# Strassen products from the third retention unit on instead of the fifth, with the first group's rows staged in DRAM

## The chip, the core and the metric

One Trainium2 chip; the program runs on one of its cores. The metric is the device time of one execution in microseconds (us). TensorE (PE) multiplies, VectorE (DVE) and ScalarE (ACT) work on the results, GpSimd (POOL) does a few small operations, and the queue of SyncE (SP) issues nearly all DMAs, in order.

## The reference, cut to what matters

A decoder trunk of two layers on x (2048 rows of 1024, float32). The first layer is gated retention with 4 heads, the second is sliding-window attention with sinks on one shared K/V. The change touches the first layer's input projection alone:

```python
def retention_layer(x, g_norm, w_in, w_out, sin, cos):
    proj = rmsnorm(x, g_norm) @ w_in
    q, k, v, gate = jnp.split(proj, [D_MODEL, 2 * D_MODEL, 2 * D_MODEL + RET_V_TOTAL], axis=-1)
    ...
    o = rms(retention(q, k, v))
    o = o.reshape(b, s, RET_V_TOTAL) * jax.nn.silu(gate)
    return x + o @ w_out
```

Per head q and k are 256 wide, v and the gate 512 wide each. `rms` makes o independent of a row's scale but for its EPS.

## The kernel before, in words

Every product is made of three: both operands are split into a high part (a cast to fp32r) and a low part (the rest), and hi·hi, hi·lo and lo·hi are summed in PSUM. ACT makes the high part and DVE the low part (`wload`, L118, for weights). A weight piece is 128 x 1024 floats, 512 KB.

`phase_a` is the retention layer. The rows lie in 4 groups of 512, and a *unit* is one group and one head, so there are 16 units, u0 to u15; u0 to u3 are the first group. The loop at its end (L802) puts `main(u+1)` (the projections of the next unit), `ret(u)` (the retention of this one) and `out_a(u)` (its share of the output product) side by side; `drive` steps two of them in a fixed ratio.

`main` computes q and k (`project_qk`, 96 matmuls of 512 columns), then v and the gate in one of two ways:

- A *plain* unit, u < PLAIN (`plain_vg`): 4 pieces for v and 4 for the gate, each used by 24 matmuls, 192 in all. The rows are not normalised; a row's scale is applied when the result leaves PSUM (`vs`, `es`, and the scale of Silu).
- A *Strassen* unit (`strassen`, L420): the 1024 x 1024 weight block and the rows are cut in 2 x 2 blocks and 7 products stand in for 8. There are 14 pieces, each used by 12 matmuls, 168 in all. Four of the seven products take sums of weight blocks (T1 to T4), and four take sums of row blocks (S1 to S4).

These sums are made beforehand, staged in DRAM, and read back:

- `stage_sums(h)` (L359) makes T1 to T4 of a head, in 4 blocks. A block loads 4 tiles (L368), subtracts and adds on DVE (L371 to L374) and writes 4 tiles (L376).
- `stage_rows(g)` (L306) makes a group's normalised rows and S1 to S4: one small product spreads the rows' scales (L315), then 4 blocks follow, each 2 tile loads (L323), 2 multiplications (L327), 4 additions of half width (L331 to L334) and 6 writes.
- `row_stats(g)` (L289) makes the scales. `load_rows` and `load_sums` read the staged rows back and split them (L345 to L347).

All tiles of the staging come from one ring of six (`stp`, tag "st"). The generators are queued in `behind`, and `step()`, called at fixed places of the projections, advances the first of them. Weights and everything that is read back share a ring of three raw tiles and rings of three for the high and low parts.

The program's order on each engine is made by a scheduler when it is built, so staging can stand earlier than the step that asked for it. After phase_a comes phase_b, the attention layer, which the change leaves alone.

Of the kernel before, what the change touches and what calls it, by code (L numbers as in the profile page):

```python
# [24 lines left out]
RH = 4  # L25
# [9 lines left out]

PSUM_BUFS = {"rr": 4, "s": 2, "f": 2}
RAW = 3
PLAIN = 4
SX = ("S2", "S3", "S1", "S4")
ST = ("T2", "T3", "T1", "T4")  # L40

# [16 lines left out]
def tile_yoco(ctx, tc, x, x_t, w_qk, w_vg, wo_a, w_kv, w_b, wo_b, ag, kvg, bg, kng, qng,  # L58
# [208 lines left out]
    def phase_a(pa):  # L267
# [8 lines left out]
        st = {}  # L276
        behind = []

        def step():
            if behind and next(behind[0], "end") == "end":  # L280
                behind.pop(0)
# [67 lines left out]
        def load_rows(g, kp):  # L349
            if kp == 0:  # L350
                st["next"] = xt_tiles(f"a{g}")
            load_part(st["next"][0][kp], st["next"][1][kp], st["rows", g][kp], f"{g}_{kp}")

        def load_sums(g, n):
            hi, lo = (xsp.tile([P, KT // 2, H], F32R, tag=f"x{hl}{n}", name=f"x{hl}_{g}_{n}") for hl in ("hi", "lo"))
            load_part(hi, lo, st["rsums", g][n], f"{g}_{n}")
            st["sum", n] = hi, lo
# [115 lines left out]
        def main(u):  # L473
            g, h = units[u]
            n = f"a{u}"
            plain = u < PLAIN
            if h == 0:
                cs = p1.tile([P, T], F32, tag="cos", name=f"cos_{n}")
                sn = p1.tile([P, T], F32, tag="sin", name=f"sin_{n}")
                st["trig"] = [cs, sn]  # L480

                def load_trig():
                    nc.sync.dma_start(cs, cos_t[:, g * T : (g + 1) * T])
                    nc.sync.dma_start(sn, sin_t[:, g * T : (g + 1) * T])

                if u:
                    load_trig()
            cs, sn = st["trig"]
            q = p1.tile([P, 2, T], F32, tag="q", name=f"q_{n}")
            k = p1.tile([P, 2, T], F32, tag="k", name=f"k_{n}")  # L490
            vhi, vlo, gate = [None] * MT, [None] * MT, [None] * MT

            def put_v(m, src, scale):
                vhi[m] = vp.tile([P, DV], F32R, tag="vhi", name=f"vhi_{n}_{m}")
                vlo[m] = vp.tile([P, DV], F32R, tag="vlo", name=f"vlo_{n}_{m}")
                nc.scalar.mul(vhi[m], src, scale)
                nc.vector.scalar_tensor_tensor(vlo[m], src, scale, vhi[m].bitcast(F32), op0=ALU.mult, op1=ALU.subtract)

            def put_gate(m, src, scale=1.0):
                gate[m] = gp.tile([P, DV], F32, tag="gate", name=f"gate_{n}_{m}")  # L500
                nc.scalar.activation(gate[m], src, AF.Silu, scale=scale)

            if h == 0:
                st["xt"] = st.pop("next", None) or xt_tiles(n)
            xt = st["xt"]
            yield from project_qk(u, xt, q, k, load_trig if u == 0 else None)
            if plain:
                yield from plain_vg(u, xt, put_v, put_gate)
            else:
                if h == 0:  # L510
                    load_sums(g, SX[3])

                def src(p):
                    name = (None, None, "T2", "T3", "T1", None, "T4")[p]
                    w = st["sums", h][name] if name else w_vg[(h,) + ((0, 0), (1, 0), 0, 0, 0, (1, 1))[p]]
                    return [w[0], w[1]]

                def evac(i, j, f, src):
                    if j:
                        put_gate(2 * i + f, src)  # L520
                    else:
                        put_v(2 * i + f, src, vd[:, h : h + 1])

                def after(p):

                    if h == RH - 1 and g + 1 < NG:
                        if p in (1, 2, 6):
                            for kp in {1: (0,), 2: (1,), 6: (2, 3)}[p]:
                                load_rows(g + 1, kp)
                        elif p:  # L530
                            load_sums(g + 1, SX[p - 3])

                yield from strassen(f"{n}v", src, xt, evac, after)
                st["es", u] = [ep[:, h : h + 1]] * MT
            st[u] = (q, k, vhi, vlo, gate, st.pop(("es", u)))
# [52 lines left out]
        def plain_vg(u, xt, put_v, put_gate):  # L588
            g, h = units[u]
            n = f"a{u}"  # L590
            xhi, xlo = xt
            last = u == PLAIN - 1
            if u == 0:
                behind.insert(0, row_stats(0))
            vs = small.tile([P, MT], F32, tag="vs", bufs=2, name=f"vs_{n}")
            es = small.tile([P, MT], F32, tag="es4", bufs=2, name=f"es_{n}")
            st["es", u] = [es[:, c : c + 1] for c in range(MT)]

            def evac_v(m, ps):
                if m == 0:  # L600

                    ms, rx = st["stats", g]
                    nc.gpsimd.tensor_tensor(vs, rx, rx, op=ALU.mult)
                    nc.gpsimd.tensor_scalar(vs, vs, vd[:, h : h + 1], None, op0=ALU.mult)
                    nc.gpsimd.tensor_scalar(es, ms, ep[:, h : h + 1], None, op0=ALU.mult)
                put_v(m, ps, vs[:, m : m + 1])

            def before_v(kp):
                step()
                if last:  # L610
                    load_sums(1, SX[kp])

            def before_g(kp):
                step()
                if last and kp:
                    load_rows(1, kp - 1)

            yield from proj(vg_pieces(h, 0), KT, xhi, xlo, False, evac_v, f"{n}v", before=before_v)
            yield from proj(vg_pieces(h, 1), KT, xhi, xlo, False,
                            lambda m, ps: put_gate(m, ps, st["stats", g][1][:, m : m + 1]), f"{n}g", before=before_g)  # L620
            if last:
                load_rows(1, 3)

        def vg_pieces(h, j):
            return [w_vg[h, kp // 2, j, kp % 2] for kp in range(KT // 2)]
# [172 lines left out]
        for _ in main(0):  # L798
            pass
        bias = bias_rows()  # L800
        todo = list(pieces_b())
        for u in range(nu - 1):  # L802

            g, h = units[u + 1]
            if u + 1 in (1, 4, 5, 6):
                behind.append(stage_sums({1: 0, 4: 1, 5: 2, 6: 3}[u + 1]))
            if h == 2 and g + 1 < NG:
                behind.append(row_stats(g + 1))
                behind.append(stage_rows(g + 1))
            if u + 1 in (8, 9, 10, 12, 13, 14):  # L810
                behind.append(stage_b(todo[:9]))
                del todo[:9]
            drive(tc, main(u + 1), ret(u), 2 if u + 1 < PLAIN else 3, 0)
            for _ in itertools.islice(bias, 2 if u >= RH else 0):
                pass
            if u < nu - 2:
                for _ in out_a(u):
                    pass
# [484 lines left out]
```

## Time and profile before

| what | value |
|---|---|
| median of 3 runs (lowest to highest) | 2477.26 us (2474.19 to 2480.29) |
| the profiled execution's own time | 2477.26 us |
| its span in the profile | 2475.5 us |
| PE busy | 2418.5 us, 11576 matmuls, 98% of the span |
| DVE busy | 1624.1 us, 66% |
| ACT busy | 1055.0 us, 43% |
| DMA moved | 499.97 MB, mean 202 GB/s |
| granted TensorE clock | 0.993 of full speed |

Busy shares are means over stages. A matmul's busy time is pipelined with the next one's, so what a matmul costs is read from the spacing of their starts. Times of rows are counted from the span's start.

### The profile page before, as it was taken

How to read it: one execution, taken by the hardware profiler on the slowest of the kernel's cores; microseconds unless marked ns; L12 is line 12 of the kernel's file. 1: busy time of each engine (PE TensorE's matmuls, PEld its weight loads, DVE VectorE, ACT ScalarE, POOL GpSimd, SP SyncE). 2: the span in 40 equal slices, each digit the busy share in tenths (PEclk: the TensorE clock that was granted, in tenths of full speed). 3: DMA queues.
4: the chain of work that ended last, by engine and by line, in shares of the span. 5: the costliest groups of instructions: out<-in, count | busy, mean ns of one | idle time of the engine just before them, and what ended most of it. 6: DMA issues, size and time to landing. Idle time of an engine off the chain costs nothing.

```text
span 2475.5 us, 32133 instructions
## 1 busy us (share of the span) xinstructions
PE 2418.5 (98%) x11576; PEld 1965.9 (79%) x11576; DVE 1624.1 (66%) x2898; ACT 1055.0 (43%) x2028; POOL 234.6 (9%) x288
## 2 busy tenths in 40 slices
PE   8999999999999999999999999999999999999997
PEld 6888778887878888887788888887687787777776
DVE  5546665787778668588667765744656566566665
ACT  4333233543536455355455543433424334334332
POOL 0000000110001020001002000022101101102010
PEclk9999999999999999999999999999999999999998
DMA  8433843589786477498548843646554674655661
GB/s 297 141 116 128 285 136 115 187 310 322 228 285 218 129 255 265 134 309 296 160 153 292 290 128 94 207 149 220 192 204 147 231 239 136 211 201 184 201 216 69
DMA packets 178075, 499.97 MB, mean 202 GB/s; under 512 B 20363, under 2 KB 32956, under 8 KB 177916
## 3 DMA queue, kind: packets, MB, share of 16 engines
q1 hardware_dynamic: 177836, 497.66, 59.8%
q8 instruction: 91, 1.49, 0.2%
q14 instruction: 68, 0.56, 0.1%
q0 software_dynamic: 80, 0.26, 0.0%
HBM read 396.11 MB, written 104.88 MB: 202 GB/s over the span
## 4 chain that ended last, share of the span: by engine, by line
PE 54%; DVE 4%; DMA 3%; ACT 1%; SPq 0%; issue 0%; POOL 0%; ACTq 0%; DVEq 0%; POOLq 0%
PE o_t L1117 3%; PE pp_ao L146 2%; PE pp_ao L147 2%; PE pp_ao L148 2%; PE s_t L1068 2%; PE pp_bo L256 2%; PE pp_bo L255 2%; PE pp_bo L257 2%; PE pT_t L1099 1%; PE qtp_b L963 1%; DVE P_t L1071 1%; DMA wlo<-in_w_b 1%; PE ot_r L726 0%; PE o_r L698 0%; PE o_r L700 0%; PE o_r L699 0%
## 5 line engine op out<-in xcount | busy, mean ns | idle before, releaser
L146 PE MATMUL pp_ao<-ohi_r,whi_ao 128*128 128x512 f32 x512 | 198.8, 392 | 6.5 <-ACT whi_ao L125 5.5
L147 PE MATMUL pp_ao<-olo_r,whi_ao 128*128 128x512 f32 x512 | 199.6, 390 | 0.0
L148 PE MATMUL pp_ao<-ohi_r,wlo_ao 128*128 128x512 f32 x512 | 194.2, 390 | 0.9 <-DVE wlo_ao L126 0.9
L1071 DVE CUSTOM_DVE_ANT_0 P_t<-s_t,bias,nsnk 128x256 f32<-128x256 f32 (+1 forms) x256 | 115.1, 472 | 89.7 <-PE s_t L1068 80.1
L1081 ACT ACTIVATE P_t<-P_t,nm_t 128x128 f32<-128x128 f32 x256 | 100.4, 394 | 117.2 <-DVE P_t L1078 114.9
L766 DVE TENSOR_TENSOR x_r<-x_r,pp_ao 128x512 f32<-128x512 f32 x128 | 86.4, 683 | 63.7 <-PE pp_ao L148 63.4
L114 POOL TENSOR_SCALAR r_o_r<-sso_r,ep 128x1 f32<-128x1 f32 x48 | 34.8, 725 | 900.9 <-ACT jo_r L720 900.9
L146 PEld LDWEIGHTS pp_ao<-ohi_r,whi_ao 128*128 128x128 f32 x512 | 96.0, 188 | 27.7 <-ACT whi_ao L125 6.7
L795 ACT CAST Shi_r<-S 128x512 fp32r<-128x512 f32 x120 | 69.9, 618 | 112.3 <-PE o_r L700 74.0
L148 PEld LDWEIGHTS pp_ao<-ohi_r,wlo_ao 128*128 128x128 f32 x512 | 96.1, 188 | 21.6 <-DVE wlo_ao L126 1.6
L147 PEld LDWEIGHTS pp_ao<-olo_r,whi_ao 128*128 128x128 f32 x512 | 96.3, 188 | 19.7
L1068 PEld LDWEIGHTS s_t<-kst,qst_b 128*128 128x128 f32 x512 | 81.9, 193 | 30.5 <-DVE nm_t L1071 11.4
L1068 PE MATMUL s_t<-kst,qst_b 128*128 128x256 f32 (+1 forms) x512 | 97.6, 296 | 8.4 <-DVE nm_t L1071 8.2
L125 ACT CAST whi_ao<-raw_ao 128x1024 fp32r<-128x1024 f32 x64 | 67.1, 1049 | 90.0 <-DMA raw_ao<-in_wo_a 21.9
L796 DVE TENSOR_TENSOR Slo_r<-S,Shi_r 128x512 fp32r<-128x512 f32 x120 | 81.0, 704 | 34.0 <-ACT Shi_r L795 33.8
L126 DVE TENSOR_TENSOR wlo_ao<-raw_ao,whi_ao 128x1024 fp32r<-128x1024 f32 x64 | 78.2, 1222 | 33.5 <-ACT whi_ao L125 33.3
L713 DVE SCALAR_TENSOR_TENSOR S<-S,dl_r 128x512 f32<-128x512 f32 x112 | 74.3, 682 | 27.9 <-PE dl_r L692 27.8
L1102 ACT COPY pTs_t<-pT_t 128x512 f32<-128x512 f32 x64 | 37.3, 583 | 121.1 <-PE pT_t L1099 120.8
L256 PE MATMUL pp_bo<-olo_t,whi_bo 128*128 128x512 f32 x224 | 88.3, 394 | 0.0
L257 PE MATMUL pp_bo<-ohi_t,wlo_bo 128*128 128x512 f32 x224 | 88.2, 394 | 0.0
L255 PE MATMUL pp_bo<-ohi_t,whi_bo 128*128 128x512 f32 x224 | 85.5, 397 | 0.5 <-ACT ohi_t L1136 0.5
L964 ACT CAST qst_b<-qtp_b 128x512 fp32r<-128x512 f32 x64 | 37.4, 585 | 84.0 <-PE qtp_b L963 83.9
(1040 smaller groups left out, 7129.5 us busy)
## 6 DMA issues: line engine op xcount, KB each, us to landing
raw_ao<-in_wo_a SPq DMA_DIRECT2D x64, 512.0 KB, 4.1
b<-in_w_vg SPq DMA_DIRECT2D x64, 256.0 KB, 4.8
res<-xmid SPq DMA_DIRECT2D x28, 512.0 KB, 4.4
whi_bo<-wo SPq DMA_DIRECT2D x28, 512.0 KB, 3.9
wlo_bo<-wo SPq DMA_DIRECT2D x28, 512.0 KB, 4.8
x_r<-in_x_t SPq DMA_DIRECT2D x16, 512.0 KB, 6.4
xin<-in_x SPq DMA_DIRECT2D x16, 512.0 KB, 3.6
xmid<-x_r SPq DMA_DIRECT2D x16, 512.0 KB, 4.9
```

The lines of the kernel that those rows point to most:

```text
L126: nc.vector.tensor_tensor(lo, raw, hi.bitcast(F32), op=ALU.subtract)
L146: nc.tensor.matmul(o, hi[:, kk, sl], xh, start=st, stop=False)
L147: nc.tensor.matmul(o, hi[:, kk, sl], xl, start=False, stop=False)
L148: nc.tensor.matmul(o, lo[:, kk, sl], xh, start=False, stop=sp)
L255: nc.tensor.matmul(o, hi[:, kk, sl], xh, start=s, stop=False)
L256: nc.tensor.matmul(o, hi[:, kk, sl], xl, start=False, stop=False)
L257: nc.tensor.matmul(o, lo[:, kk, sl], xh, start=False, stop=e)
L766: nc.vector.tensor_tensor(t, t, ps, op=ALU.add)
L796: nc.vector.tensor_tensor(lo, src[:, d, :], hi.bitcast(F32), op=ALU.subtract)
L1068: nc.tensor.matmul(o, q[:, h, :], kst[:, kv * 2 + hl, kb + b0 : kb + 2, :], start=hl == 0, stop=hl == 1)
L1071: nc.vector.tensor_tensor_reduce(out=pt[:, j, :w], in0=o, in1=bias[:, kv * GQ + h, b0 * P :], scale=-1.0, scalar=nsnk[:, kv * GQ + h : kv ...
L1081: nc.scalar.activation(pt[:, i, :P], pt[:, i, :P], AF.Exp, scale=-1.0, bias=nm[:, i : i + 1], accum_out=den[:, i : i + 1])
```

## The change

PLAIN goes from 4 to 2: u2 and u3 use Strassen's products. So the first group, too, is normalised and summed in DRAM: `stage_rows(0)` is queued behind `row_stats(0)` in u0, where each step of the gate now advances the staging twice. u1 ends with the staged rows of its own group in place of the raw ones (`load_rows`, `load_sums` with g, not 1). The T sums are queued for heads 2, 3, 0, 1 in u1, u2, u3, u4, where before they were queued for heads 0 to 3 in u1, u4, u5, u6. `drive` steps u2 and u3 three to one against the retention, as it does Strassen units, where it was two to one.

```diff
-PLAIN = 4
+PLAIN = 2
...
-            if h == 0:
+            if u == 0 or "next" in st:
                 st["xt"] = st.pop("next", None) or xt_tiles(n)
...
             if u == 0:
-                behind.insert(0, row_stats(0))
+
+                behind[:0] = [row_stats(0), stage_rows(0)]
...
             def before_v(kp):
                 step()
                 if last:
-                    load_sums(1, SX[kp])
+                    load_sums(g, SX[kp])
 
             def before_g(kp):
-                step()
+                for _ in range(2 if u == 0 else 1):
+                    step()
                 if last and kp:
-                    load_rows(1, kp - 1)
+                    load_rows(g, kp - 1)
...
             if last:
-                load_rows(1, 3)
+                load_rows(g, 3)
...
-            if u + 1 in (1, 4, 5, 6):
-                behind.append(stage_sums({1: 0, 4: 1, 5: 2, 6: 3}[u + 1]))
+            if u < RH:
+                behind.append(stage_sums((2, 3, 0, 1)[u]))
```

SP's queue in u1, from the first gate piece (a1g) to the first piece of the output product (ao0). Names: raw is a weight piece, b2 and b3 are blocks of heads 2 and 3 (head, block, place), T1v to T4v are their sums on the way to DRAM, xb_0 is a staged row tile read back. Before:

```order
L122 DMA raw_a1g_0_1205<-in_w_vg 128x1024
L122 DMA raw_a1g_1_1235<-in_w_vg 128x1024
L122 DMA raw_a1g_2_1265<-in_w_vg 128x1024
L735 DMA Sd0_165<-S32_0_659 128x1024
L122 DMA raw_a1g_3_1295<-in_w_vg 128x1024
L122 DMA raw_ao0_0_0_1337<-in_wo_a 128x1024
```

And in the change, between the third and the fourth gate piece:

```order
L122 DMA raw_a1g_2_1394<-in_w_vg 128x1024
L368 DMA b3_1_00_1793<-in_w_vg 128x512
L368 DMA b3_1_01_1794<-in_w_vg 128x512
L376 DMA T3v_3_1714<-b3_0_11_1720 128x512
L376 DMA T1v_3_1715<-b3_0_01_1718 128x512
L376 DMA T2v_3_1713<-b3_0_00_1717 128x512
L368 DMA b3_1_10_1795<-in_w_vg 128x512
L368 DMA b3_1_11_1796<-in_w_vg 128x512
L345 DMA xb_0_2_1424<-xn2_0_523 128x1024
L376 DMA T4v_3_1716<-b3_0_10_1719 128x512
L368 DMA b3_2_00_1918<-in_w_vg 128x512
L376 DMA T3v_3_1714<-b3_1_11_1796 128x512
```

Five more DMAs follow before raw_a1g_3. Where one DMA stood between those two weight pieces, 16 stand now, and writes among them wait for DVE.

DVE's order at the same place (wlo is the low part of a weight piece, vlo that of v, xlo that of a row tile). Before:

```order
L497 SCALAR_TENSOR_TENSOR vlo_a1_3_1198<-pp_a1v_3_994,vs_a1_989,vhi_a1_3_1197 128x512
L126 TENSOR_TENSOR wlo_a1g_2_1268<-raw_a1g_2_1265,whi_a1g_2_1267 128x1024
L126 TENSOR_TENSOR wlo_a1g_3_1298<-raw_a1g_3_1295,whi_a1g_3_1297 128x1024
L126 TENSOR_TENSOR wlo_ao0_0_0_1340<-raw_ao0_0_0_1337,whi_ao0_0_0_1339 128x1024
L126 TENSOR_TENSOR wlo_ao0_0_1_1370<-raw_ao0_0_1_1367,whi_ao0_0_1_1369 128x1024
```

In the change:

```order
L126 TENSOR_TENSOR wlo_a1g_2_1397<-raw_a1g_2_1394,whi_a1g_2_1396 128x1024
L374 TENSOR_TENSOR b3_0_10_1719<-b3_0_10_1719,b3_0_00_1717 128x512
L371 TENSOR_TENSOR b3_1_11_1796<-b3_1_11_1796,b3_1_01_1794 128x512
L372 TENSOR_TENSOR b3_1_01_1794<-b3_1_01_1794,b3_1_00_1793 128x512
L373 TENSOR_TENSOR b3_1_00_1793<-b3_1_11_1796,b3_1_00_1793 128x512
L374 TENSOR_TENSOR b3_1_10_1795<-b3_1_10_1795,b3_1_00_1793 128x512
L347 TENSOR_TENSOR xlo_a0_0_1344<-xb_0_0_1348,xhi_a0_0_1340 128x1024
L347 TENSOR_TENSOR xlo_a0_1_1345<-xb_0_1_1390,xhi_a0_1_1341 128x1024
L371 TENSOR_TENSOR b3_2_11_1921<-b3_2_11_1921,b3_2_01_1919 128x512
L126 TENSOR_TENSOR wlo_a1g_3_1431<-raw_a1g_3_1428,whi_a1g_3_1430 128x1024
```

The fourth gate piece's low part stands behind the first operation of block 2 of head 3, the eleventh block of staging since the start.

SP's queue in u3, where v and the gate are now Strassen's (a3v), and staging of heads 0 and 1 (b0, b1) stands among the pieces:

```order
L122 DMA raw_a3v_01_2866<-in_w_vg 128x1024
L368 DMA b0_2_01_3083<-in_w_vg 128x512
L376 DMA T3v_0_2909<-b0_1_11_3023 128x512
L376 DMA T1v_0_2910<-b0_1_01_3021 128x512
L376 DMA T2v_0_2908<-b0_1_00_3020 128x512
L368 DMA b0_2_10_3084<-in_w_vg 128x512
L376 DMA T4v_0_2911<-b0_1_10_3022 128x512
L368 DMA b0_2_11_3085<-in_w_vg 128x512
L368 DMA b0_3_00_3141<-in_w_vg 128x512
L368 DMA b0_3_01_3142<-in_w_vg 128x512
L122 DMA raw_a3v_10_2890<-in_w_vg 128x1024
```

Nine DMAs of staging stand between the second and the third piece there.

## Rows read from the trace of the kernel before

**Rows 1.** The page's head and its section 1 (busy us, share, count).

```profile
span 2475.5 us, 32133 instructions
PE 2418.5 (98%) x11576; PEld 1965.9 (79%) x11576; DVE 1624.1 (66%) x2898; ACT 1055.0 (43%) x2028; POOL 234.6 (9%) x288
```

**Rows 2.** Windows from one unit's first q/k matmul to the next's; the first is u0.

```profile
core 0: us, PE busy (x) PEld busy (x) DVE busy (x) ACT busy (x) POOL busy (x), PEclk, DMA share, GB/s
7.40:79.70 72.30, 70.33 (x308) 57.55 (x308) 41.64 (x53) 28.21 (x36) 4.65 (x10) 1.00 0.87 298
79.70:184.90 105.20, 105.20 (x486) 87.25 (x484) 54.99 (x71) 37.52 (x54) 5.96 (x11) 1.00 0.31 103
184.90:289.70 104.80, 104.20 (x478) 85.88 (x476) 66.30 (x101) 34.40 (x50) 5.62 (x11) 1.00 0.59 192
289.70:400.70 111.00, 106.96 (x490) 87.63 (x488) 70.65 (x91) 41.64 (x57) 4.75 (x8) 1.00 0.51 166
400.70:499.90 99.20, 99.20 (x459) 82.34 (x458) 69.78 (x85) 48.76 (x73) 12.59 (x14) 1.00 0.50 161
499.90:610.20 110.30, 107.37 (x495) 87.51 (x494) 88.44 (x121) 48.21 (x74) 14.27 (x15) 1.00 0.89 306
610.20:708.40 98.20, 96.36 (x435) 78.30 (x433) 73.06 (x108) 42.82 (x61) 2.84 (x6) 1.00 0.80 265
708.40:816.90 108.50, 107.30 (x495) 88.34 (x496) 86.33 (x114) 59.86 (x90) 8.83 (x12) 1.00 0.67 219
```

**Rows 3.** Timeline of PE in u1 and u2 (start us, us, engine, line, operation).

```profile
117.66 0.39 PE L152 MATMUL pp_a1v<-whi_a1v,xlo_a 128*128 128x512 f32 x1
...
120.84 0.39 PE L150 MATMUL pp_a1v<-whi_a1v,xhi_a 128*128 128x512 f32 x1
...
237.97 1.02 PE L315 MATMUL rpx<-dgx,ones 128*128 128x512 f32 x2
238.83 0.49 PE L726 MATMUL ot_r<-ident_r,gate_a 128*128 128x128 f32 x3
```

**Rows 4.** Groups of DVE's instructions, 0 to 900 us (busy us, mean ns | idle before).

```profile
L126 DVE TENSOR_TENSOR wlo_a5v<-raw_a5v,whi_a5v 128x1024 fp32r<-128x1024 f32 x14 | 16.9, 1218 | 3.4 <-ACT whi_a5v L125 3.4
...
L371 DVE TENSOR_TENSOR b<-b,b 128x512 f32<-128x512 f32 x16 | 11.1, 691 | 35.4 <-DMA b<-in_w_vg 30.3 <-DMA T4v<-b 3.3 <-issue 1.7
...
L347 DVE TENSOR_TENSOR xlo_a<-xb,xhi_a 128x1024 fp32r<-128x1024 f32 x8 | 9.8, 1223 | 13.9 <-ACT xhi_a L346 13.9
...
L331 DVE TENSOR_TENSOR xss<-xst,xst 128x256 f32<-128x256 f32 x8 | 3.4, 421 | 0.1
```

**Rows 5.** Timeline of DVE in u0: three staging blocks begin; v's last low part.

```profile
46.29 0.69 DVE L371 TENSOR_TENSOR b<-b,b 128x512 f32<-128x512 f32 x1 [4.13 <-DMA b<-in_w_vg]
...
55.92 0.69 DVE L371 TENSOR_TENSOR b<-b,b 128x512 f32<-128x512 f32 x1 [3.61 <-DMA b<-in_w_vg]
...
60.31 0.74 DVE L497 SCALAR_TENSOR_TENSOR vlo_a<-pp_a0v,vs_a,vhi_a 128x512 fp32r<-128x512 f32 x1
...
65.59 0.69 DVE L371 TENSOR_TENSOR b<-b,b 128x512 f32<-128x512 f32 x1 [3.40 <-DMA b<-in_w_vg]
```

**Rows 6.** Timeline of DVE in u5: staging blocks of head 2 begin.

```profile
536.74 0.68 DVE L371 TENSOR_TENSOR b<-b,b 128x512 f32<-128x512 f32 x1
537.34 0.68 DVE L584 TENSOR_TENSOR k_a<-k_a,th_a 128x512 f32<-128x512 f32 x1
...
552.27 0.68 DVE L371 TENSOR_TENSOR b<-b,b 128x512 f32<-128x512 f32 x1
...
569.25 0.68 DVE L371 TENSOR_TENSOR b<-b,b 128x512 f32<-128x512 f32 x1
```

**Rows 7.** Timeline of PE where u5's output product begins.

```profile
583.26 0.50 PE L146 MATMUL pp_ao<-ohi_r,whi_ao 128*128 128x512 f32 x1 [2.63 <-ACT whi_ao L125]
```

**Rows 8.** DMA issues (count, KB each, us from issue to landing).

```profile
b<-in_w_vg SPq DMA_DIRECT2D x64, 256.0 KB, 4.8
...
T1v<-b SPq DMA_DIRECT2D x16, 256.0 KB, 3.6
```

## The prediction

> **What bounds the kernel now.** First the page's head and busy line: the span is 2475.5 us and PE is busy for 98% of it [rows 1]. Busy time of pipelined matmuls proves little by itself, so the timeline of PE comes next: in u1 fourteen steps from one product's start to the next take 120.84 less 117.66, 0.227 us each, with no idle named among them [rows 3]. Then the windows by unit, where a window's length less its PE busy time is PE's idle time [rows 2]: 2.0 us in u0, then 0, 0.6, 4.0, 0, 2.9, 1.8 and 1.2 us in u1 to u7, 12.5 us in 810. So phase_a is bound by PE, and a matmul taken out is worth its 0.227 us as long as nothing new makes PE wait. The granted clock is 1.00 in every window, that is 2.4 GHz throughout. The profiled execution took 2477.26 us, 1.8 us more than its span; the median of the runs is the same 2477.26, so differences carry over as they are. What a measurement can tell from no change is about 0.3%, 7.4 us.
>
> **The change, part by part.**
>
> *Matmuls.* u2 and u3 go from 192 products to 168 each: 48 fewer, at 0.227 us 10.9 us. The small product of `stage_rows(0)` is added, two instructions that together hold PE from 237.97 to 238.83, 0.9 us [rows 3]. It stands between v and gate of u0, where PE has work on both sides. Net 10.0 us less. All else on PE is the same work at another place.
>
> *DVE and ACT.* Each of the two units has 6 more weight pieces (1.22 us each on DVE) and 6 additions of full width, 0.69 us as the blocks' own: 11.4 us a unit. `stage_rows(0)` adds 16 half additions of 0.42 us, 8 multiplications and some small ones, about 15 us, and reading the rows back 8 splits of 1.22 us [rows 4]. Together some 47 us of DVE durations. They overlap: an operation of 0.68 us is followed 0.60 us later [rows 6], so I count each instruction of DVE's order at its row's duration less 0.08 us, from a unit's first weight piece to the next unit's. Before that gives 51, 64, 68, 65, 88, 73, 86 us for u1 to u7, which fits the windows' 55, 66, 71, 70, 88, 73, 86 [rows 2]; for the change it gives 87, 74, 92, 58, 71, 77, 76. About 70 us move into or appear in u1 to u3, and some 30 us leave u4 to u7. Hidden, this costs nothing, since a unit of PE takes 98 us or more. But u3 with 92 us would be DVE's fullest unit.
>
> *DMA.* The change moves 15.9 MB more (sizes of SP's rows added up). What counts is where: SP's rows from u1's first weight piece to u2's carry 34.9 MB (13.9 before), and those of u3 33.8 MB (22.8 before), while u5 falls from 34.1 to 21.9 MB. The fullest unit before is u5 at 306 GB/s, with the DMA engines 0.89 busy [rows 2].
>
> *New waits in u1.* From its first to the next unit's first product PE has 109.6 us of matmuls there. At u5's 306 GB/s the 34.9 MB take 114.1 us, 4.5 us more. The second reading is the ring of six. In u0, where blocks follow each other as fast as they can, they begin 9.6 to 9.7 us apart, and DVE stands waiting 3.4 to 4.1 us for each [rows 5]; all sixteen blocks together made DVE idle for 35.4 us [rows 4]. A load of 4.8 us must follow a write of 3.6 us into the same tile [rows 8]. In the change eleven blocks precede the low part of u1's last gate piece. The first begins near 62 us, when the last low part of u0's v is done [rows 5]. At 9.7 us a block, or DVE's own work between two of them where that is longer, the eleventh begins near 161 us and the low part is ready near 163; PE has 77 us of matmuls from the unit's start to it and, starting at 79.7 as before [rows 2], wants it near 157. That is 6 us. The bound below is 0: in u1 before, DVE's waits of u0 cost PE nothing. I take 4.5 us, since u5 is the only stretch before with this load.
>
> *New waits in u3.* From the low part of v's first piece to that of the output product's first piece DVE has 63.1 us of work, PE between the first uses of these two 52.1 us. In u5 before, the same two sums are 58.0 and 52.9, an excess of 5.1 us, and PE then waited 2.6 us [rows 7]. The excess of 11.0 is 5.9 more, so 8.5 us. By DMA: 33.8 MB at 306 GB/s are 110.5 us, against 102 us of matmuls, 8.5 us as well. Bounds: 2.6 us, if it is no worse than u5, and 11 us, the whole excess.
>
> By the Trainium skill (DMA: Bandwidth & Descriptors, Bandwidth) the memory gives a core about 358 GB/s, and a single core with large transfers has reached 425. By 358 the two units' bytes would take 97.5 and 94.4 us, less than PE's matmuls, and DMA would add no wait at all; that is the world of the first rival below. No row here shows a unit over 306 GB/s.
>
> *Waits that go.* u5 loses its staging (88 to 71 us of DVE, 34.1 to 21.9 MB), so of its 2.9 us I leave 0.5. u3's 4.0 us came with a row of eight blocks and are replaced by the 8.5. u0 loses its four weight blocks and gets the rows' blocks later, after v has left PSUM: 0.5 of 2.0. u2 gets 1.0 for 0.6. u4, u6 and u7 I leave at 0, 1.8 and 1.2.
>
> *Smaller parts.* At the end of u1 the row tiles are overwritten with the normalised ones before u2 starts; before, u3 did the same for u4, and u4 shows no idle time [rows 2], so 0; if that cover goes, u2 starts later by one piece's landing. Six small POOL operations vanish from an engine busy for 9% [rows 1]: 0. From u9 on the orders of PE and DVE hold the same pieces with the same work between them: 0.
>
> *Sum.* Idle in u0 to u7 becomes 0.5 + 4.5 + 1.0 + 8.5 + 0 + 0.5 + 1.8 + 1.2 = 18.0 us where it was 12.5, so 5.5 us come back of 10.0: 4.5 us faster, **2472.8 us**, 0.2%, inside what a measurement can tell. The unknown terms' bounds (0 to 6 and 2.6 to 11) put this case between 2462 and 2477; I keep 2469 to 2477 for it and give the lower part to the next case.
>
> **The rivals.**
>
> *The staging hides.* DVE and the DMA engines take the load, as in u1 before, where PE had no idle time though blocks of head 0 still ran. For it: the mean over u1 to u3 is 284 GB/s and 84 us of DVE a unit, which u5 already bears. Against: the two full units are full by order, since SP does not overtake. Then the first group idles no more than the 6.6 us it did, u5 gives 2.4 back, and the time is 2477.3 − 10.0 − 2.4 = 2465 us.
>
> *The ring turns slower than 9.7 us, and the change loses.* SP issues in order, DVE works in order, and the weights of u1 stand among the blocks in both. If loads land later under the fuller queue, each block's delay adds to the next: eleven blocks have ten turns, so each further 1 us a turn makes u1's last gate piece 10 us later, and PE waits for it. In u5 the blocks began 15.5 and 17.0 us apart [rows 6], though there the scheduler had spread them. It decides at about 10.2 us a turn, where 5 us more eat the gain; at 10.7 u1 loses 10 us more and u3, with eight blocks ahead of its v, some 4: 2472.8 + 14 = 2487 us. Against it: u0's turns of 9.6 to 9.7 us were run with DMA 0.87 busy over that window [rows 2, 5].
>
> The Trainium skill (Perfetto Trace Analysis, Identifying the Most-Contended Engine and the strategy after it) says that the same gap repeating can mean too few buffers for the next tile. The waits of 4.1, 3.6 and 3.4 us agree, and the change puts twelve blocks into u0 and u1, where there were four.
>
> **How the numbers follow.** Forecast 0.45, hiding 0.32, slow ring 0.23. Faster by over 7.4 us means below 2469.9: nearly all of the hiding case and a ninth of the forecast, 0.35. Slower by over 7.4 us means above 2484.7: some two thirds of the slow ring, 0.16. The rest, 0.49, is within 0.3%. The range holds the forecast, the hiding case down to 2463 and the slow ring up to 2487; about 0.1 lies below and as much above.
>
> **What the profile of the changed kernel would show.** Matmul records near 11530. PE idle of 3 to 6 us in u1, ended by ACT or DVE on gate pieces or the output product's first pieces, 6 to 11 us in u3 at Strassen pieces, under 1 us in u5. GB/s over 300 in u1 and u3. L371 about 9.7 us apart in u1 with DVE waiting for b. If u3's waits stay under 3 us the hiding case is right; if L371 comes 11 us apart or more and u1 idles for over 12 us, the slow ring is. The prediction is wrong at its root if the products of u2 and u3 no longer start 0.227 us apart, or if idle time appears after u8.

## The result and the profile after

The change takes **2489.29 us** (median of 7 runs, 2484.51 to 2497.61) against 2477.26 us (7 runs, 2473.42 to 2484.93): a ratio of 1.0045, 95% interval 1.003 to 1.006. It is 12 us slower, and 2.3 us outside the range that was given.

The profiled execution took 2484.51 us and is the fastest of the seven; its mean granted clock was 0.992, the other six had 0.988 to 0.991. So the rows below can explain some 7 us of the 12. The rest lies in executions of which only spans and clocks are known; their clock is lower, which points the same way but shows no more.

The head of the page, to be held against [rows 1]:

```profile
span 2482.7 us, 32241 instructions
PE 2414.1 (97%) x11530; PEld 1960.3 (79%) x11530; DVE 1661.2 (67%) x2958; ACT 1078.1 (43%) x2059; POOL 232.8 (9%) x282
```

The windows by unit, u0 to u7, against [rows 2] (the columns are those of that group):

```profile
core 0: us, PE busy (x) PEld busy (x) DVE busy (x) ACT busy (x) POOL busy (x), PEclk, DMA share, GB/s
7.30:78.70 71.40, 70.79 (x307) 57.44 (x307) 41.91 (x60) 28.33 (x36) 3.73 (x8) 1.00 0.75 250
78.70:203.00 124.30, 115.31 (x516) 94.49 (x515) 91.12 (x126) 45.33 (x64) 9.89 (x10) 0.96 0.80 262
203.00:306.30 103.30, 99.97 (x459) 82.24 (x458) 72.32 (x108) 47.28 (x71) 7.07 (x12) 1.00 0.64 211
306.30:423.60 117.30, 108.98 (x478) 87.52 (x478) 94.80 (x127) 48.54 (x68) 8.68 (x11) 0.97 0.80 271
423.60:513.90 90.30, 90.30 (x412) 75.05 (x411) 60.43 (x72) 43.72 (x61) 7.67 (x7) 1.00 0.52 165
513.90:619.40 105.50, 105.50 (x486) 86.76 (x484) 72.64 (x94) 49.86 (x75) 10.06 (x13) 1.00 0.64 218
619.40:716.60 97.20, 97.14 (x445) 80.11 (x444) 74.06 (x112) 45.98 (x70) 5.47 (x8) 1.00 0.72 246
716.60:825.00 108.40, 106.50 (x492) 87.36 (x491) 81.61 (x103) 55.73 (x80) 6.86 (x12) 1.00 0.59 194
...
80.00:180.00 100.00, 91.01 (x404) 74.36 (x404) 74.30 (x103) 37.98 (x55) 8.69 (x9) 0.95 0.86 282
```

Read as the prediction read them (length less PE busy): PE idles 0.6, 9.0, 3.3, 8.3, 0, 0, 0.1 and 1.9 us, 23.2 us in all, where it was 12.5. And the clock column, 1.00 in every window of before, shows 0.96 in u1 and 0.97 in u3. The eight units take 817.7 us instead of 809.5. The balance: −10.0 of products, +10.7 of idle time, and 7.5 us that only the clock can hold. Length times missing clock gives 124.3 × 0.04 + 117.3 × 0.03 = 8.5 us. That is a little more, since part of the low clock fell into a wait, where it costs nothing: over 160 to 180 us the granted clock was 0.83, which misses 20 × 0.17 = 3.4 us, while the products there lost 2.2 us, as counted below. From u8 on the rest takes 1657.7 us against 1658.6: unchanged.

The timeline of PE at the two long waits of u1 shows wait and clock together; the last two lines are the two longest waits of u3:

```profile
96.21 0.39 PE L571 MATMUL pp_a1qk<-xhi_a,wlo_a1qk 128*128 128x512 f32 x1
99.43 0.63 PE L728 MATMUL ot_r<-ident_r,gate_a 128*128 128x128 f32 x4 [2.83 <-DVE gate_a L725]
...
161.05 0.60 PE L671 MATMUL kt_r<-ident_r,k_a 128*128 128x128 f32 x4
167.30 2.08 PE L150 MATMUL pp_a1g<-whi_a1g,xhi_a 128*128 128x512 f32 x4 [5.65 <-ACT whi_a1g L125]
169.18 0.63 PE L151 MATMUL pp_a1g<-wlo_a1g,xhi_a 128*128 128x512 f32 x1
169.60 0.63 PE L152 MATMUL pp_a1g<-whi_a1g,xlo_a 128*128 128x512 f32 x1
...
171.74 0.49 PE L152 MATMUL pp_a1g<-whi_a1g,xlo_a 128*128 128x512 f32 x1
172.06 0.39 PE L150 MATMUL pp_a1g<-whi_a1g,xhi_a 128*128 128x512 f32 x1
...
337.45 0.47 PE L451 MATMUL pp_a3vb<-whi_a3v,xhi_a 128*128 128x512 f32 x1 [2.05 <-DVE th_a L581]
...
361.71 0.63 PE L728 MATMUL ot_r<-ident_r,gate_a 128*128 128x128 f32 x4 [2.40 <-DVE gate_a L725]
```

After 5.65 us of idle the products start 0.43 us apart until 172.06, then 0.23 again: the lower of the clock's two levels, 1.2 GHz, for 4.8 us, 2.2 us lost beyond the wait. There are four such stretches in u0 to u7, at 99, 167, 339 and 362 us, each after waits. Counted by the spacing of products of 512 columns, the first three lose about 1.7, 2.2 and 1.6 us; the fourth holds mostly smaller products. u1's 9.0 us of idle time are the 2.83 and 5.65 us shown here and 0.51 us at 88 us.

What DVE did ahead of these two, in its timeline:

```profile
92.40 0.69 DVE L371 TENSOR_TENSOR b<-b,b 128x512 f32<-128x512 f32 x1 [4.09 <-DMA b<-in_w_vg]
...
98.54 0.74 DVE L725 SCALAR_TENSOR_TENSOR gate_a<-o_r,r_o_r,gate_a 128x512 f32<-128x512 f32 x1
...
155.64 0.69 DVE L371 TENSOR_TENSOR b<-b,b 128x512 f32<-128x512 f32 x1 [3.99 <-DMA b<-in_w_vg]
...
166.80 0.69 DVE L371 TENSOR_TENSOR b<-b,b 128x512 f32<-128x512 f32 x1 [6.02 <-DMA b<-in_w_vg]
```

And SP, and ACT behind it:

```profile
142.96 0.42 SPq L122 DMA_DIRECT2D raw_a1g<-in_w_vg  x1
...
156.36 0.32 SPq L376 DMA_DIRECT2D T3v<-b  x1
...
159.73 0.55 SPq L122 DMA_DIRECT2D raw_a1g<-in_w_vg  x1
```

```profile
166.20 1.04 ACT L125 CAST whi_a1g<-raw_a1g 128x1024 fp32r<-128x1024 f32 x1 [10.68 <-DMA raw_a1g<-in_w_vg]
```

Ahead of 99 us DVE stands 4.09 us for a staging load, and the gated output that PE wants is behind that block in DVE's order. At 167 us it is SP's order: a store of T waits for the first operation of DVE's block (155.64), the last gate weights of u1 stand behind it and are asked for at 159.73, 16.8 us after the piece before, and arrive 6.5 us later.

### The profile page after: what moved, and what is told of

Same layout as the page of the kernel before. It is cut to its first block, busy times and chain, and to the rows that moved or that the text cites. A ratio compares the mean times of both kernels' runs of the same rounds, so it can differ in the third digit from the quotient of the medians.

```text
span 2482.7 us, 32241 instructions
## 1 busy us (share of the span) xinstructions
PE 2414.1 (97%) x11530; PEld 1960.3 (79%) x11530; DVE 1661.2 (67%) x2958; ACT 1078.1 (43%) x2059; POOL 232.8 (9%) x282
## 5 line engine op out<-in xcount | busy, mean ns | idle before, releaser
L1070 PEld LDWEIGHTS s_t<-kst,qst_b 128*128 128x128 f32 x512 | 81.6, 193 | 30.7 <-DVE nm_t L1073 11.7
```

What stands on the lines that cost most here:

```text
L1070: nc.tensor.matmul(o, q[:, h, :], kst[:, kv * 2 + hl, kb + b0 : kb + 2, :], start=hl == 0, stop=hl == 1)
```

## The experiments

Theory A: the staging of group 0, crowded into u1 and u3, stands ahead of what PE needs in SP's and DVE's orders; PE waits, and after the waits its clock is low. Theory B: the new Strassen products cost what they save. Others are named where they come up. Edits are against the change unless said otherwise. Each ratio is to runs of the kernel before on the same chip, whose medians lay between 2476.87 and 2477.92 us.

**Products alone.**

```diff
-                behind[:0] = [row_stats(0), stage_rows(0)]
+                behind.insert(0, row_stats(0))
...
-                behind.append(stage_sums((2, 3, 0, 1)[u]))
+                behind.append(stage_sums({1: 0, 4: 1, 5: 2, 6: 3}[u + 1]))
...
+                    if g == 0 and name:
+                        return [w_vg[h, 0, 0, 0], w_vg[h, 0, 0, 1]]
```

> The change's products alone: u2 and u3 are multiplied in Strassen's way with the change's splits and additions, but heads 2 and 3 and the rows of group 0 are not staged for them. Left out is that part of the computation: group 0's row sums are read from parts of x, and its weight sums from one plain piece of the same size, so pieces and bytes read are those of the change. Staging for the later groups stands where it stood before. Theory A: 48 products fewer come back in full, 2477.3 - 10.9 = about 2466 us, waits in u1 under 1 us, in u3 no more than the 4 us of before. Theory B: PE waits 8 to 12 us in u3 all the same and 2477 us or more comes out.

This kernel leaves out the staging for u2 and u3, so its result is not the whole one. Measured: 2471.68 us, ratio 0.998 (0.9969 to 0.9992). u1 to u3:

```profile
82.20:189.50 107.30, 106.79 (x489) 87.77 (x488) 65.04 (x81) 45.38 (x63) 5.01 (x8) 1.00 0.42 139
189.50:289.10 99.60, 99.60 (x458) 82.29 (x457) 75.85 (x111) 43.89 (x62) 6.03 (x10) 1.00 0.67 225
289.10:399.00 109.90, 106.34 (x489) 86.52 (x488) 84.89 (x110) 51.52 (x74) 8.58 (x12) 1.00 0.59 199
```

Waits of 0.5, 0 and 3.6 us, clock 1.00: the products with their splits and additions fit in, as A says, and B falls. Its units u0 to u7 take 801.7 us, 7.8 less than before; the median gains 5.4 us of the 10.9 that A had put down.

**Staging alone** (against the kernel before).

```diff
-                behind.insert(0, row_stats(0))
+                behind[:0] = [row_stats(0), stage_rows(0)]
...
-            if u + 1 in (1, 4, 5, 6):
-                behind.append(stage_sums({1: 0, 4: 1, 5: 2, 6: 3}[u + 1]))
+            if u < RH:
+                behind.append(stage_sums((2, 3, 0, 1)[u]))
```

> The kernel before, with the staging of the change alone: the rows of group 0 and the sums of heads 2 and 3 are staged in u0 and u1 (the order of heads 2, 3, 0, 1, two staging steps per piece in u0's gate and all through u2), but u2 and u3 keep their 192 plain products and read nothing of it. Theory A: u1 loses what it loses in the change, 7 to 10 us of PE waits and some 4 us of low clock, so 2477.3 + 1 + 13 = about 2491 us, and nothing is given back by fewer products. Theory B: staging hides beside u1, 2476 to 2480 us, all of the change's loss is in u2 and u3.

Measured: 2483.49 us, ratio 1.0025 (1.0012 to 1.0039). u1 to u3:

```profile
79.10:189.90 110.80, 107.11 (x485) 87.68 (x484) 75.78 (x108) 33.88 (x49) 4.99 (x11) 0.98 0.76 254
189.90:304.50 114.60, 107.35 (x484) 87.87 (x482) 66.49 (x100) 38.52 (x56) 5.32 (x11) 0.99 0.56 180
304.50:417.60 113.10, 109.04 (x487) 88.75 (x488) 82.42 (x109) 40.47 (x55) 4.53 (x8) 0.98 0.72 242
```

Staging costs time with no product changed, 6 us, but about half of what A expected, and not where A had it: u1 waits 3.7 us here and 9.0 in the change, where the row tiles and sums (4 MB) are read back in the same unit, while u2 waits 7.3 us (0.6 before). Together the two halves make +1 us (−5.4 and +6.4), the change +12: the parts do not add up, so the rest comes from having both at once.

**Head 3's blocks moved behind the rows of group 1.**

```diff
+            if u in (0, 2, 3):
+                behind.append(pause((0, 0, 6, 0)[u]))
                 behind.append(stage_sums((2, 3, 0, 1)[u]))
...
+            if u == 1:
+                behind.append(stage_sums(3))
```

> The change, with the sums of head 3 put behind the rows of group 1 in the row of staging work, and six empty steps ahead of the sums of head 0; products, bytes and operations stay those of the change, only the place of sixteen blocks moves. Theory A (crowding, and the clock after it): in the change the blocks of heads 2 and 3 stand in SP's row ahead of u1's gate weights, PE waits 3.0 and 5.8 us in u1, and its products start 0.43 instead of 0.23 us apart for some 4 us after each wait (1.9 us lost each time). With only head 2's blocks left in u1 these go: 2489.3 - 9 - 4 = about 2476 us, granted clock 1.00 over 80 to 200 us; waits in u3 stay, about 12 us. Theory B (the products of u2 and u3 themselves, with their splits, additions and rows read back, cost what they save): no change, 2486 to 2492 us.

Measured: 2477.08 us, ratio 1.0011 (0.9999 to 1.0022). u1 and u3, and PE's longest wait:

```profile
78.80:190.60 111.80, 108.67 (x494) 89.58 (x493) 77.96 (x105) 44.39 (x62) 6.26 (x8) 0.98 0.67 220
290.10:416.50 126.40, 113.13 (x503) 90.74 (x502) 100.32 (x136) 52.66 (x77) 14.39 (x14) 0.96 0.82 277
```

```profile
324.65 0.77 PE L455 MATMUL pp_a3va<-whi_a3v,xhi_a 128*128 128x512 f32 x1 [6.67 <-DVE th_a L585]
```

DVE ahead of it:

```profile
322.61 0.69 DVE L375 TENSOR_TENSOR b<-b,b 128x512 f32<-128x512 f32 x1 [5.51 <-DMA b<-in_w_vg]
...
323.82 0.68 DVE L585 TENSOR_TENSOR th_a<-pp_a3qk,sin_a 128x512 f32<-128x512 f32 x1
```

With nothing but the place of the blocks changed, 12 us come back: A's number. u1 is 12.5 us shorter, as A had it, and waits 3.1 us (the one at 99 us stays, which A did not expect). But the waits of u3 grow to 13.3 us, since head 3's blocks now reach into it: DVE's rotation of q and k stands behind them and behind the next block, for whose load DVE waits 5.51 us. That unit is 9.1 us longer. So A is right on u1, and its total is in part luck: u0 to u7 together are only 4.5 us shorter and the two profiled executions 7.6 us apart, where the medians differ by 12.2.

**Extra products in the wait.** 26 and then 52 products of which nothing is read stand ahead of u1's last gate piece.

```diff
+            if name == "a1g" and kp == 3:
+                jk = bank("jk_a1g")
+                for i in range(26):
+                    nc.tensor.matmul(jk, xhi[0][:, 0, :P], hi[:, i % 2, :], start=i == 0, stop=i == 25)
```

> The change, with 26 extra products (results unread, 5.9 us at 0.227 us each) in PE's order right ahead of u1's last gate piece, for which PE waited 5.65 us at 167 us. Everything else is the change's. Theory A (the clock falls because PE stood idle): after the piece arrives products start 0.227 us apart at once, granted clock 1.00 over 160 to 180 us where the change had 0.83; the fall after the wait at 99 us stays. Total 1 to 3 us less than the change, 2486 to 2489 us. Theory C (the clock falls there for another reason, such as the full DMA queues): products stand 0.43 us apart around 167 to 172 us as in the change, 2489 us or a little more.

> As the run with 26 extra products ahead of u1's last gate piece, with 52 of them (11.8 us), more than the whole time until the piece arrived there (9.6 us after its forerunner's last product). Results of the extra products are not read. Theory A (the clock falls because PE stood idle): no wait is left there, the products after it start 0.227 us apart at once and the granted clock is 1.00 from 140 to 180 us; the fall after 100 us stays. Theory C (something else lowers it): products 0.43 us apart at 170 to 176 us even without a wait. The time is not the question: 2 to 4 us more than the change.

Measured: 2489.9 us with 26, ratio 1.0055 (1.0035 to 1.0074). The piece came later, 3.36 us of wait remained, and the clock over 160 to 180 us was 0.83 as in the change: no answer. With 52 (2498.7 us, 1.0087 (1.0064 to 1.0109); in u3 a wait of 9.9 us) the wait is covered:

```profile
159.85 11.95 PE L138 MATMUL jk_a1g<-whi_a1g,xhi_a 128*128 128x512 f32 x52
171.63 0.39 PE L154 MATMUL pp_a1g<-whi_a1g,xhi_a 128*128 128x512 f32 x1
171.86 0.39 PE L155 MATMUL pp_a1g<-wlo_a1g,xhi_a 128*128 128x512 f32 x1
```

```profile
160.00:180.00 20.00, 18.55 (x86) 15.33 (x85) 9.69 (x13) 5.08 (x6) 0.00 (x0) 1.00 0.85 292
```

The clock is 1.00 and the products 0.23 us apart at once, with the DMA engines as busy as in the change. At this place the clock fell because PE stood idle, and not because the DMA engines were full. The three other falls were not tried in this way.

**Staging issued by POOL.** The loads and stores of the blocks go from `nc.sync` to `nc.gpsimd`.

```diff
-                        nc.sync.dma_start(b[i][j], vg[i, j, c // 2, :, c % 2, :])
+                        nc.gpsimd.dma_start(b[i][j], vg[i, j, c // 2, :, c % 2, :])
...
-                    nc.sync.dma_start(dt[c // 2, :, c % 2, :], t)
+                    nc.gpsimd.dma_start(dt[c // 2, :, c % 2, :], t)
```

> The change with the loads and stores of the weight blocks issued by POOL instead of SP; bytes, DVE work and products stay. Theory E (SP's row is what holds u1's weights: stores that wait for DVE stand ahead of weight loads): the weights are asked for in time, u1's wait at 167 us falls from 5.7 to under 1.5 us, b is in DVE's hands as late as before, and the time is 2480 to 2484 us unless POOL's own small operations for the retention come late, which would show as waits for r_o_r. Theory F (the DMA engines carry no more than 280 to 290 GB/s of this mix): the wait stays within 2 us of the change's at that piece or moves to u1's next pieces, the GB/s over 80 to 180 us stay under 295, and the time is 2487 to 2492 us.

Measured: 2487.89 us, ratio 1.004 (1.0025 to 1.0055). u1:

```profile
78.40:196.30 117.90, 111.19 (x506) 89.66 (x505) 86.26 (x120) 44.88 (x63) 42.29 (x74) 1.00 0.79 265
```

The wait at 167 us is gone and u1 is 6.4 us shorter: SP's order made that wait. But the rate stays where it was (265 GB/s, 262 in the change), waits of 1.2 to 2.1 us appear at 98 to 113 us, among them the rotation behind staging in DVE's order, and u3 takes 122.9 us where the change took 117.3. The Trainium skill (DMA: Bandwidth & Descriptors, Issuing engines are not separate DMA queues) says that all issuers share the same 16 engines and that several of them save only the time to issue. The rate agrees; that the one wait went shows that a row of waiting issues can cost more than that.

**Half of the change.**

```diff
-PLAIN = 2
+PLAIN = 3
...
+            if u == 0:
+                behind.append(stage_sums(3))
...
+            if 0 < u < RH:
+                behind.append(stage_sums(u - 1))
```

> Half of the change: only u3 has Strassen's products, u2 stays plain, the rows of group 0 are read back in u2, and the sums are staged in the order of heads 3, 0, 1, 2. 24 products fewer than before, 5.4 us. Theory A: u1 holds four weight blocks and no rows read back, so it waits at most the 3 us at 99 us; u3 waits as in the change, 9 us with 4 us of low clock after, against 4.5 and 1.8 before: 2477.3 - 5.4 + 1 + 3 + 2 + 6.5 = about 2484 us, or 2477 if u3 is relieved by u2. Theory B (each Strassen unit of group 0 costs its share of the loss): half of the change's loss, 2483 us, with the waits in u3 alone.

Measured: 2478.48 us, ratio 1.0004 (0.9994 to 1.0014). 24 products fewer, 5.4 us, bring nothing either: u3 waits again, 5.45 us of it for the rotation behind the blocks.

**Empty steps ahead of every head.**

```diff
+                behind.append(pause((4, 6, 10, 3)[u]))
                 behind.append(stage_sums((2, 3, 0, 1)[u]))
...
-                step()
+                step(2 if n == "a2v" and p > 1 else 1)
```

> The change with the staging spread further: four empty steps ahead of the sums of head 2, six ahead of head 3's, ten ahead of head 0's, three ahead of head 1's, and two staging steps a time in the second part of u2, so that the rows of group 1 are staged in time. Products, operations and bytes are the change's; in DVE's order two blocks stand ahead of u1's last gate piece that come from head 3 (three in the change), the first block of head 2 comes later, the rows of group 1 reach into u3, and head 1's blocks stand in u4 and u5. Theory A (crowding, and the clock after each wait): all waits of u1 and u3 shrink and none of 2.5 us or more is left, so the low clock goes too; the products' 10 us come back down to the rest of u3 and u7: 2468 to 2474 us. Theory D (in u3 any staging costs, since DVE has no room beside that unit's own work): u1 is mended as in the run with head 3's blocks moved, u3 keeps 10 us or more of waits, and the time is 2475 to 2481 us.

Measured: 2495.88 us, ratio 1.0071 (1.0058 to 1.0084). A miss for both theories: the scheduler takes the blocks early anyway (DVE begins head 2's first at 97.5 us and head 3's at 150.7, where the change has 92.4 and 146.1), waits of 3.1 and 3.0 us for weights came in u1 (100 and 175 us), and one of 4.48 us for a gated output in u5, where head 1's blocks now stand in DVE's order.

**The ring held back.** Small POOL writes take the six staging tiles until q of a unit is done; then the next blocks may start.

```diff
+        def hold():
+            st["hold"] = [stp(f"hold_{i}") for i in range(6)]
+            for t in st["hold"]:
+                nc.gpsimd.memset(t[:, :1], 0.0)
+            yield
...
+                for t in st.pop("hold"):
+                    nc.gpsimd.tensor_copy(t[:, :1], q[:, 1, :1])
+                if u == 2:
+                    behind.extend([stage_sums(3), row_stats(1), stage_rows(1), hold()])
```

> The change, with the staging held back by its own tiles: after head 2's blocks the six tiles of the ring are taken by small POOL writes and given free only when u2's q is done; then head 3 and the rows of group 1 follow (two staging steps a time in u2), the ring is taken again until u3's q is done, then head 0, and again until u4's q, then head 1. In DVE's order u1 has head 2's four blocks, u2 head 3's four and the rows' four, u3 head 0's four from its v on, u4 head 1's four. Products, bytes and DVE work are the change's, some 36 small POOL operations are added. The two runs that moved blocks by empty steps showed that the scheduler still takes their loads early, into the end of u1 or the start of u3. Theory A (crowding): u1 waits as in the first of those, 3.5 us, u2 1 us, u3 5 us, the low clock is about before's, and nearly all of the products' 10 us comes through: 2468 to 2473 us. Theory D (each staged block costs PE the same wherever it stands): 2477 us or more, with new waits of several us in u2 or u4.

> As the run with the staging held back, and head 2's blocks held back too, until u1's q is done. In DVE's order the first block of head 2 then stands behind u0's gated outputs, for which PE waited 3.0 us at 99 us. Theory A: that wait and the low clock after it go, 3 + 1.8 us less than the run held in u2 to u4 alone, 2464 to 2469 us, unless u1's gate pieces now find the blocks ahead of them. Theory D: no difference to that run beyond 2 us.

Measured: 2503.53 us (1.0103, 1.0088 to 1.0118) and 2511.36 us (1.0134, 1.0117 to 1.0151), far worse. In the first, SP, PE and ACT:

```profile
230.37 0.38 SPq L122 DMA_DIRECT2D raw_a2v<-T2v  x1
...
262.25 0.32 SPq L122 DMA_DIRECT2D raw_a2v<-T3v  x1
```

```profile
268.22 1.22 PE L458 MATMUL pp_a2vb<-whi_a2v,xhi_S 128*128 128x512 f32 x2 [22.69 <-ACT whi_a2v L125]
```

```profile
261.07 1.06 ACT L305 ACTIVATE jx<-xin 128x1024 bf16<-128x1024 f32 x1 [14.92 <-DMA b<-in_w_vg]
```

Set free at once, four blocks and the statistics of group 1, whose inputs share the weights' buffers, stand between two weight pieces: 31.9 us from one request to the next, and PE waits 22.69 us, at four blocks in u2, no more than u1 of the moved run bore well. The statistics also hold what the weights need: their inputs fill the ring of three raw tiles, their squares (jx) take tiles of the staging ring, and the first of them runs only at 261.07 us, so the next weight piece is asked for at 262.25. So neither the number of blocks in a unit nor their bytes decide alone, but what holds up the next weight piece, in SP's order or in its buffers; the run does not part these two. The time is in theory D's range (2477 us or more), but by this one wait, not by a price for each block. In the second run PE waits 19.66 us at the same place, and u1 waits 8.2 us, though the wait at 99 us, at which that run aimed, falls to 1.22 us. Its time is outside what either theory expected.

**The ring held at two other places**: after head 2's blocks until u1's first gate row, and until u3's q ahead of head 0.

```diff
+                behind.extend([stage_sums(2), hold()])
+            elif u == 1:
+                behind.extend([stage_sums(3), row_stats(1), stage_rows(1), hold()])
...
+                for t in st.pop("hold"):
+                    nc.gpsimd.tensor_copy(t[:, :1], st["gate"][:, :1])
```

> The change, with the ring taken by small writes at two places: after head 2's blocks until u1's first gate row is out, and after the rows of group 1 until u3's q is done. In DVE's order: u1's last gate piece, then head 3's blocks around u2's q and k, the rows of group 1 in u2, head 0's blocks in u3 from the third product on, head 1's at the end of u3 and in u4. The burst of the runs held to u2's q (31 staging transfers between two of u2's weight pieces, 22.7 us of waiting) should not come back, since head 3 is done before the statistics of group 1 ask for a tile of the ring. Theory A (a weight piece is late when staging transfers stand ahead of it in SP's row, so few blocks a unit are cheap): u1 waits 3.5 us, u2 2 us, u3 6 to 8 us, 2470 to 2476 us. Theory D (staging costs PE its share wherever it stands in group 0): 2477 to 2485 us, with the waits moved to u2.

Measured: **2474.41 us** (12 runs), ratio 0.9989 (0.9975 to 1.0003). u1 to u4:

```profile
79.40:191.30 111.90, 107.80 (x494) 88.11 (x494) 82.53 (x112) 43.05 (x60) 8.82 (x20) 1.00 0.76 256
191.30:295.60 104.30, 104.04 (x480) 85.46 (x479) 82.05 (x122) 48.37 (x71) 7.50 (x18) 1.00 0.70 232
295.60:410.00 114.40, 108.10 (x482) 87.76 (x480) 88.58 (x117) 50.41 (x73) 15.26 (x18) 0.97 0.75 253
410.00:505.50 95.50, 92.47 (x412) 76.01 (x411) 65.74 (x80) 43.45 (x61) 7.68 (x7) 0.98 0.62 203
```

The same products and bytes as the change, and some 15 us less, as A expected and D did not; the intervals of the two ratios do not touch. Waits are 4.1, 0.3, 6.3 and 3.0 us, and the clock in u1 and u2 is 1.00. The profiled executions are 7.8 us apart, all of it in u0 to u7. Against the kernel before 2.9 us is no certain gain; it is the best version that computes the whole result.

**More weight buffers, fewer staging tiles**: `RAW = 4`, and `bufs=4` for the tag `st` everywhere.

> The change, with four buffers for weight pieces instead of three and four staging tiles instead of six (the same memory): a weight piece can be asked for one piece earlier, a block's loads only when the block before is written out. Theory A (what counts is that weight loads stand behind staging in SP's row): waits for weight pieces in u1 and u3 shrink, the one at 167 us from 5.7 to under 3 us, blocks come 12 us or more apart, and the time falls to 2478 to 2486 us. Theory F (the DMA engines' rate for this mix is the limit): PE waits as much for the later blocks' units, 2488 to 2495 us, with 280 GB/s over 80 to 180 us as in the change.

Measured: 2502.73 us, ratio 1.01 (1.0076 to 1.0124). That is outside what either theory expected. The wait at 167 us is gone, and u1 takes 117.1 us where the change took 124.3; but from u8 on the time is 1680.9 us where the change took 1657.7. Later stages use the staging tiles too; that these two fewer are what costs them the 23 us is likely, not shown. The run supports what POOL's showed of the wait at 167 us, and is no way out.

## Why the prediction was wrong

The profiled execution, 2484.51 us, missed the forecast of 2472.8 us by 11.7 us, with the products' 10.0 us counted as forecast. Two steps failed: the clock, which had no term in the sum (7.5 us), and the idle time (23.2 us for 18.0).

The larger step is the clock. "The granted clock is 1.00 in every window, that is 2.4 GHz throughout" was read for u0 to u7 [rows 2] and carried over to a kernel with longer waits. Four falls cost some 7.5 us, by the balance above. The Trainium skill (TensorE: Matmul & The Clock Gate, HAM oscillation) describes this: waits for DMA between groups of products send the clock to half. The wait at 167 us agrees, and the run with 52 products takes the low clock there away. Without the four falls the profiled execution would have come to 2477 us, no change at all. The trace of before had the warning outside the windows that were read: there the clock was 0.95 over 1160 to 1180 us and 0.93 over 1200 to 1220 us, behind waits of 1.1 to 2.0 us.

The other step is the term for u1: "At u5's 306 GB/s the 34.9 MB take 114.1 us, 4.5 us more", with 6 us as the upper bound. Measured were 9.0 us, and 3.3 us in u2 for 1.0. The wait that the term meant, the one for the last gate piece, came much as the ring's reading had it, 5.65 us for 6. In part that is luck: the fifth block since the start, head 2's first, begins at 92.4 us, where 62 us and four turns of 9.7 us give 100.8; from there the blocks turn more slowly, and the eleventh begins at 166.8 us for 161, while PE stands at the piece from 161.65 us for 157. What the term lacked is the wait at 99 us, 2.83 us, for an output of u0 behind head 2's first block in DVE's order: the sum priced u1 by its bytes and by one late piece, not by each thing that stands behind a block.

Nor was u5 the nearest row for the bytes. u1's window carried 262 GB/s (32.6 MB; some of the 34.9 MB run ahead of it), and 282 GB/s over 80 to 180 us. At 282 GB/s the 34.9 MB would take 123.8 us, and u1 took 124.3; but that rate holds the waits in it, so it restates the time and does not explain it. The 306 GB/s came from a stretch in which the scheduler had placed the blocks further apart; in u1 stores wait for DVE, DVE for loads, and SP for both.

The other points in order:
- Products: right. 11530 records, and the balance holds with 10.0 us less of them; the run with products alone had its shorter units. Behind the four falls products of u1 and u3 did not start 0.227 us apart, which the prediction had named, for u2 and u3, as a sign of being wrong at its root.
- DVE work hides: right in size (91, 95 and 73 us in u1, u3 and u5 for 87, 92 and 71 forecast), but its order decides, not its sum: the waits at 99 us and for the rotation in u3 are for operations that stand behind a block whose load is late.
- u3: 8.3 us for 8.5, right in size, and in part by luck. The prediction had 6 to 11 us at Strassen pieces; 2.3 us stood there, 2.4 for a gated output, 2.1 for the rotation and 1.0 at the output product. The clock, 0.97, had no term here either.
- u5 to u7: 0, 0.1 and 1.9 us for 0.5, 1.8 and 1.2, right in sum but for 1.5 us.
- GB/s over 300 in u1 and u3: wrong, 262 and 271.
- Nothing after u8: right.
- The rivals: "the ring turns slower" has 2487 us, nearest to what came, and one of its two signs. The blocks of u1 begin 11.5, 11.2, 17.2, 13.8, 9.5 and 11.2 us apart, 12.4 on average, beyond the 10.2 named as the point of decision. But u1 idles 9.0 us, not over 12, and the 10 us in u1 for each further 1 us a turn did not come. It had no term for the clock either, so that its number is near is luck. It was given 0.23 on the strength of u0's turns of 9.6 to 9.7 us [rows 5], where no rows were read back between the blocks. In the run with staging alone, where u1 reads no rows back either, the same seven blocks begin 10.4 us apart (95.31 to 157.72 us).

What stays open: how the six executions without a profile lost their further 1 to 13 us, and how much of u1's low rate is order and how much the DMA engines' own limit. The runs show that order alone is worth 12 to 15 us in the medians, some 8 us of it in the profiled executions, not that a better order would reach the 2471.68 us of the products alone.

## What to carry to other kernels

Price a new transfer by what will stand behind it in its issuer's and its consumers' orders, and take a rate from a stretch with the same spacing of dependent loads and stores, not from the one with the highest GB/s. Give each new wait of several us of a busy TensorE a second price, that of the slow products after it. When a saving fails to show, move the added work before giving up the idea: the same products and bytes here cost between 2474 and 2511 us by place, with some small POOL writes in the runs that held the ring.

## What was unexpected

One late piece cost twice: the 5.65 us wait and 2.2 us of slow products. Shorter waits differ: after the 2.83 us at 99 us the clock was low, after 2.63 us in u5 before [rows 7] it was 1.00. In the run with 52 extra products that earlier wait was 2.23 us, and the clock stayed 1.00 over 100 to 120 us, where the change has 0.91.
